# A fused encoder layer on one core: another order in the front, and more places for gate weights, projection weights and tanh tiles

## The chip, the cores and the metric

The kernel runs on one core of a Trainium2 chip. The metric is the device time of one execution in microseconds; times given are medians of several executions. A core has TensorE (PE in the profile), VectorE (DVE), ScalarE (ACT), GpSimd (POOL) and SyncE (SP). Each takes its own instructions in the order in which they were written for it; they wait for each other by semaphores. SP and ACT also issue the transfers (DMA): an issue is an instruction in that engine's order, and what stands behind it waits until the issue may go out.

## What is computed

One layer of a streaming encoder in fp32, for 1024 prompt rows and 8 x 16 sampled rows together (1152 rows of 1024):

```python
z = rmsnorm(x) @ w_in                       # q,k,v of branches a and b, q of m, forget gate, 3 x 1024 gates
a: band attention, 8 heads x 64, bias by distance
b: forgetting attention, 8 heads x 64, logit[t, s] += sum of log sigmoid(forget gate)
m: cross attention to 256 memory tokens, 4 heads x 128
x += (sum over branches of sigmoid(gate) * (branch @ w_p)) @ w_o
x += relu(rmsnorm(x) @ w_up) ** 2 @ w_down
```

It returns the layer's output, the normed keys, the values and the log forget gates.

## The kernel before

Each fp32 operand of a matmul is split in a hi part (rounded to fp32r, mostly by ScalarE) and a lo part (the difference, mostly by VectorE), and each product is three matmuls: hi by hi, hi by lo, lo by hi. Before a product can start on TensorE, its weight or left side must be loaded raw, copied to hi, and subtracted to lo.

The stages in order of time:

- **Front (0 to 75 us).** x is loaded transposed in five tiles of 256 rows (the fifth, tile 4, of 128; its output tile is number 8, `TT - 1`) into an arena FE (`x_place`, `x_load`, L375 to L381), split (`x_split`, L383), and multiplied with the weights of branch a's values and of the forget gate (loop at L750). `x_place` has two places of 2048 columns that take turns, and one of 1024 for tile 4. Beside it the rows of x are loaded once more, 512 KB at a time, into FE from column 4096, and squared and summed by ScalarE for the norm (`row_sums`, L393; `x_rows`, L399). After every second output tile, `sums` (L421) adds halves of x for the products that follow, and only then does the code load, split and row-sum the next tile.
- **Input projections (75 to 369 us).** q, k, v of a and b and q of m in products that share sums of operands (seven in place of eight). Raw weights go through a ring of slots in an arena RW; `kept` are four of them that are loaded in the front.
- **Memory keys and values (356 to 390 us).** `mem_products` (L823) with two output tiles; `flush` runs what is due of delayed steps (`in_`, L558), and `odd_x` (L801) prepares the right side for later. `norm` (L593) squares, sums and scales the keys, `to_T` transposes them on TensorE.
- **Attention (395 to 1090 us).** Written by a planner (class `Plan`, L50): a heap of steps with estimated due times and costs for each engine. The order of all engines from here is what this plan comes to, so an added buffer or another estimate moves everything behind it. Attention to the prompt and to the samples, aa, sa, ab, sb, am, sm, is done in turn. Where TensorE would wait, the plan puts in filler: first `gates` (L936), 24 products with weights in_w_g over three column tiles of 384, whose tanh goes to a table tg in DRAM; then `merge`.
- **Gates' weights.** `staged` (L924) loads a weight with a DMA that ACT issues into a raw tile `wst`, copies hi (`whi`) and subtracts lo (`wlo`). There is one raw tile for the gates. `get(f + 1)` is called at the gate's second column tile (L965).
- **Merge (957 to 1172 us).** For each branch (a, b, m), eight weights in_w_p and three column tiles, four slices each: products `z<-hi,whi` with the attention output (oTa, oTb, oTm, read back by SP and split in `load` and `part`, L995 to L1014), multiplied with the tanh tiles `th`, which SP reads back from tg through three places (`tanhs`, L985). The weights go through a ring "st" of three. The first two weights are asked for once gate 22 has begun its last column tile (`weights`, L1050).
- **Forget gates.** `forget_gates` (L849): log sigmoid in some 25 small VectorE steps, a transpose (tp<-lf), two running sums, both to DRAM; branch b reads them from 650 us on.
- Then the output projection (1172 to 1280), and the MLP (up to 1650, down to 2009 us).

The wait of the merge's first weights and the one raw tile for the gates, as written:

```python
yield from plan.until(lambda: ("x", 22, 2) in late and "mf" in late)     # merge, weights()
def staged(pool, src, tiles, at, key, shape=(P, 512), ring=("wst", 1)):
wq = fil.enter_context(weights(1, 4, "wq", "right"))                     # one raw tile, four split ones
```

## Time and profile before

| | us |
|---|---|
| median of 3 runs | 2014.13 |
| lowest and highest | 2010.42, 2015.04 |
| profiled execution, its own time | 2010.68 |
| span of that execution in the trace | 2008.9 |
| mean granted clock of TensorE | 0.989 of full speed |

In the rows below, a row of a timeline is one instruction or several alike (x4): its start and duration in us, engine, line, operation, output and inputs by the program's names, and in brackets how long its engine was idle before it and whom it waited for. Most instructions carry the line of a helper (L203, L215, L222), so they are told by the names of the tiles. A row of DMA on a queue (SPq, ACTq) is the issue; when the data has landed is seen from the instruction that reads it. A window's row gives length, busy time of PE, PEld (weight loads), DVE, ACT and POOL, then the granted TensorE clock, the busy share of the DMA engines and what they moved.

### The profile page before, as it was taken

What the parts mean: (1) busy time and instruction counts of PE and PEld (TensorE: products, weight loads), DVE (VectorE), ACT (ScalarE), POOL (GpSimd) and SP (SyncE); (2) the same over time, 40 slices, a digit from 0 to 9 for tenths busy, and PEclk for the clock granted to TensorE, in tenths of its full rate; (3) what the DMA queues carried; (4) which work ended last, traced back from release to release, by engine and by line L of the source; (5) the groups of instructions that cost most, each with busy time, mean ns of one, the idle gap of its engine ahead of it and who ended that gap; (6) DMA issues with size and microseconds to landing.
All of it is one profiled execution on the core that took longest, in us unless ns stands there. A gap on an engine that the chain in (4) does not pass through costs nothing.

```text
span 2008.9 us, 33955 instructions
## 1 busy us (share of the span) xinstructions
PE 1954.7 (97%) x12338; PEld 1712.1 (85%) x12338; DVE 1221.4 (61%) x2313; ACT 946.0 (47%) x1831; POOL 521.1 (26%) x590
## 2 busy tenths in 40 slices
PE   8999999899999999998899999999999999999999
PEld 8887888788887988887898987889999998888887
DVE  7766657665632555522575843876666665785775
ACT  6645556455643556533452313644444454453332
POOL 3343433332311244311122200244443431000000
PEclk9999999999999999999898999999999999999999
DMA  8555455643259433278658453144343459563463
GB/s 264 162 156 180 117 168 150 203 152 102 80 164 316 154 104 98 68 245 278 196 179 282 153 162 113 46 157 157 127 141 129 143 169 330 183 197 106 128 197 126
DMA packets 223909, 330.54 MB, mean 165 GB/s; under 512 B 32357, under 2 KB 109302, under 8 KB 223742
## 3 DMA queue, kind: packets, MB, share of 16 engines
q1 hardware_dynamic: 166600, 270.44, 42.3%
q10 hardware_dynamic: 57142, 57.93, 8.7%
q8 instruction: 97, 1.59, 0.3%
q14 instruction: 70, 0.57, 0.1%
HBM read 243.11 MB, written 85.18 MB: 163 GB/s over the span
## 4 chain that ended last, share of the span: by engine, by line
PE 77%; DMA 10%; DVE 6%; ACT 2%; issue 2%; POOL 2%; SPq 1%; ACTq 0%; POOLq 0%; DVEq 0%
PE b L1863 36%; PE z L215 28%; PE tp L222 5%; PE tp L215 4%; PE s L215 4%; DMA wst<-in_w_g 2%; DMA th<-tg 1%; POOL fa L203 1%; DVE r L203 1%; DVE fa L203 1%; DVE lo L203 1%; DMA kd<-in_cak 1%; DMA fa<-in_w_up 1%; SPq L203 1%; DMA tg<-tg 1%
## 5 line engine op out<-in xcount | busy, mean ns | idle before, releaser
L1863 PE MATMUL b<-r 128*128 128x512 f32 (+2 forms) x2200 | 457.6, 357 | 4.2 <-ACT r L203 2.1
L1863 PEld LDWEIGHTS b<-r 128*128 128x128 f32 x2200 | 379.6, 190 | 62.6 <-DVE r L203 3.6
L203 ACT ACTIVATE r<-fa 128x512 fp32r<-128x512 f32 (+4 forms) x264 | 212.8, 816 | 327.2 <-PE b L1863 280.9
L203 DVE TENSOR_TENSOR r<-fa,r 128x512 fp32r<-128x512 f32 (+4 forms) x264 | 273.5, 1047 | 136.1 <-ACT r L203 131.9
L215 PE MATMUL z<-hi,whi 128*128 128x384 f32 x960 | 320.2, 365 | 15.0 <-ACT hi L203 8.0
L1863 PE MATMUL b<-r,r 128*128 128x320 f32 (+1 forms) x1928 | 288.3, 299 | 5.8 <-DVE r L203 5.7
L1863 PEld LDWEIGHTS b<-r,r 128*128 128x128 f32 x1928 | 271.2, 190 | 7.7 <-DVE r L203 7.7
L215 PE MATMUL z<-hi,wlo 128*128 128x384 f32 x768 | 262.0, 341 | 0.2
L203 POOL TENSOR_TENSOR fa<-fa 128x512 f32<-128x512 f32 x114 | 165.2, 1455 | 238.4 <-ACT fa L203 125.5
L215 PEld LDWEIGHTS z<-hi,whi 128*128 128x128 f32 x960 | 180.5, 193 | 39.4 <-issue 15.1
L215 PE MATMUL z<-wa,hi 128*128 128x512 f32 (+1 forms) x732 | 203.5, 365 | 6.4 <-ACT hi L203 4.7
L215 PE MATMUL z<-lo,whi 128*128 128x384 f32 x576 | 195.1, 339 | 0.0
L215 PEld LDWEIGHTS z<-wa,hi 128*128 128x128 f32 x732 | 128.7, 192 | 27.2 <-ACT hi L203 5.1
L215 PEld LDWEIGHTS z<-hi,wlo 128*128 128x128 f32 x768 | 146.7, 191 | 1.3 <-DVE wlo L203 1.3
L203 ACT ACTIVATE s<-s,nm 128x256 f32<-128x256 f32 (+8 forms) x180 | 121.2, 679 | 39.1 <-DVE nm L203 38.9
L203 POOL TENSOR_SCALAR s<-s,ri 128x256 f32<-128x256 f32 (+8 forms) x108 | 76.0, 709 | 232.1 <-DVE ri L203 208.7
L215 PE MATMUL z<-wa,lo 128*128 128x512 f32 (+1 forms) x366 | 130.5, 359 | 0.0
L203 DVE CUSTOM_DVE_ANT_0 s<-s,bias 128x384 f32<-128x384 f32 (+4 forms) x144 | 70.4, 526 | 84.3 <-PE s L215 81.3
L215 PEld LDWEIGHTS z<-lo,whi 128*128 128x128 f32 x576 | 109.8, 191 | 0.0
L222 PE MATMUL tp<-ident,s 128*128 128x128 f32 (+1 forms) x680 | 107.3, 277 | 1.7 <-ACT pt L203 1.2
L203 ACT ACTIVATE pt<-tp 128x256 f32<-128x256 f32 (+3 forms) x153 | 66.4, 454 | 80.6 <-PE tp L222 76.8
L203 DVE TENSOR_TENSOR fa<-b,fa 128x256 f32<-128x256 f32 (+1 forms) x160 | 70.5, 448 | 54.0 <-PE b L1863 39.1
(223 smaller groups left out, 3136.4 us busy)
## 6 DMA issues: line engine op xcount, KB each, us to landing
td<-fa SPq DMA_DIRECT2D x112, 256.0 KB
rw<-in_w_in SPq DMA_DIRECT2D x104, 256.0 KB
fa<-td SPq DMA_DIRECT2D x80, 256.0 KB
fa<-in_w_down SPq DMA_DIRECT2D x76, 256.0 KB
fa<-in_w_up SPq DMA_DIRECT2D x32, 512.0 KB
tg<-tg ACTq DMA_DIRECT2D x72, 192.0 KB
th<-tg SPq DMA_DIRECT2D x72, 192.0 KB
wst<-in_w_g ACTq DMA_DIRECT2D x48, 256.0 KB
```

What stands on the lines that cost most here:

```text
L203: ins = f(*a, **k)
L215: ins = nc.tensor.matmul(out, lhsT, rhs, **k)
L222: ins = nc.tensor.transpose(*a)
L1863: pin(nc.tensor.matmul(ps, lh, rh, **k))
```

## The change

In the front: a third place for x tiles (`t % 3`); the rows of x go to the arena RW, whose slots are not used yet, and to FE only for the last ones; tile 4 is loaded and split ahead of the first row sums; tile 2 is loaded, row-summed and split after output tile 0; the kept weights, rows 4 and 5, tile 3 and the first raw weights come after output tile 1. At the memory: the square goes to another tile; delays of 3 instead of 2; `odd_x` makes its parts with scaled splits, four ScalarE and four VectorE steps per tile, in steps 2 to 5 instead of at every second one. The forget gates start 30 us later by the plan, their VectorE estimate is 6 us instead of 3, the running sums are done in place. The gates have two raw tiles, and each asks for the next at its first column tile. The merge's first two weights have tiles of their own, and are asked for as soon as the pool "mf" is there; the tanh tiles have six places. The attention's twelve minima are columns of one tile.

```diff
@@ -375,7 +375,7 @@
         return FE[:, 4096:5120].rearrange("p (k t) -> p k t", k=8) if t == 4 else \
-            FE[:, t % 2 * 2048:t % 2 * 2048 + 2048].rearrange("p (k t) -> p k t", k=8)
+            FE[:, t % 3 * 2048:t % 3 * 2048 + 2048].rearrange("p (k t) -> p k t", k=8)
     def x_load(t, ks=slice(0, 8)):
@@ -391,7 +391,7 @@
     def row_sums(src, s, r, e):
-        xt = FE[:, 4096 + e * D:4096 + e * D + D]
+        xt = row[1][:, e * D:e * D + D]
         sp.dma_start(xt, src)
@@ -401,7 +401,7 @@
             row[0] = 1 - row[0]
-    row = [1]
+    row = [1, RW]
@@ -590,11 +590,11 @@
                 flush()
-    def norm(z, sc, dh, then, gain=None, fresh=False):
+    def norm(z, sc, dh, then, gain=None, fresh=False, lag=2):
         nh = HB // dh
         v3 = lambda t: t.rearrange("p (h d) -> p h d", h=nh)
-        sq = tl(pj, (P, HB), tag="sq", bufs=1)
+        sq = tl(pj, (P, 4, P), tag="zt").rearrange("p k t -> p (k t)") if fresh else tl(pj, (P, HB), tag="sq", bufs=1)
         act.activation(sq, z, AF.Square, scale=sc)
@@ -603,7 +603,7 @@
             gps.tensor_scalar(r[:, :nh], r[:, :nh], sc, 1.0, ALU.mult, ALU.mult)
-            in_(2, scale)
+            in_(lag, scale)
         def scale():
@@ -644,8 +644,8 @@
             sp.dma_start(o["mk"][t * P:(t + 1) * P, :], zn)
-            in_(2, lambda: to_T(zn, mkT, t))
-        norm(z, rm[:, t:t + 1], 128, then, g_of["km"], True)
+            in_(3, lambda: to_T(zn, mkT, t))
+        norm(z, rm[:, t:t + 1], 128, then, g_of["km"], True, 3)
     mem_v = v_out(o["mv"], rm, True)
@@ -721,12 +721,12 @@
         x_split(0, (k,))
-    x_rows(0)
-    sp.dma_start(bf, i["b_f"].to_broadcast((P, 8)))
     x_load(4)
     x_split(4)
+    x_rows(0)
     x_load(1, slice(0, 4))
     x_load(1, slice(4, 8))
+    sp.dma_start(bf, i["b_f"].to_broadcast((P, 8)))
     x_rows(1)
@@ -735,8 +735,6 @@
     makers.extend([take] * 16)
-    for k in range(4):
-        sp.dma_start(kept[k], rows_(Q_A)(k))
     sp.dma_start(ident, i["ident"])
@@ -762,21 +760,30 @@
         vec.scalar_tensor_tensor(lf[:, t, :], z[1][:, 252:260], rs[:, t:t + 1], bf, ALU.mult, ALU.add)
+        if t == 0:
+            x_load(2, slice(0, 4))
+            x_load(2, slice(4, 8))
+            x_rows(2, 3)
+            x_split(2)
         if t in (1, 3, 5):
...
                 step()
-            if t < 5:
-                x_load(t // 2 + 2, slice(0, 4))
-                x_load(t // 2 + 2, slice(4, 8))
-                x_split(t // 2 + 2)
-                x_rows(t + 1, t + 2)
             if t == 1:
+                for k in range(4):
+                    sp.dma_start(kept[k], rows_(Q_A)(k))
+                row[1] = RW[:, 6 * UW:]
+                x_rows(4, 5)
+                x_load(3, slice(0, 4))
+                x_load(3, slice(4, 8))
                 ask()
+                x_split(3)
             if t == 3:
+                row[1] = FE[:, 2048:4096]
                 x_rows(6, 7)
+    row[1] = FE[:, 4096:6144]
     for t in range(2):
         row_sums(i["mem"][t * P:(t + 1) * P, :], ss[:, TT + t:TT + t + 1], rm[:, t:t + 1], t)
-    T2, u2, u3 = ([FE[:, (4 * j + t) * HB:(4 * j + t + 1) * HB] for t in range(4)] for j in range(3))
+    u2, u3, T2 = ([FE[:, (4 * j + t) * HB:(4 * j + t + 1) * HB] for t in range(4)] for j in range(3))
     sp.dma_start(tri, i["tri"])
@@ -801,8 +808,9 @@
         x = kept[t].rearrange("p (k t) -> p k t", k=4)
-        vec.tensor_tensor(x, x, gcol[:, 0, 0:4, None].to_broadcast((P, 4, P)), ALU.mult)
-        into_odd(t, x)
+        h, l = odd(t)
+        for k in range(4):
+            hilo_scaled(x[:, k, :], h[:, k, :], l[k], gcol[:, 0, k:k + 1])
     def at_last(t):
@@ -831,10 +839,12 @@
             release(u0 + k)
-            if k % 2:
+            if u0 != 104:
                 flush()
-                if u0 == 104:
-                    odd_x(k // 2)
+            elif k % 2:
+                flush()
+            if u0 == 104 and 1 < k < 6:
+                odd_x(k - 2)
         for t in range(2):
@@ -848,6 +858,7 @@
     def forget_gates(pool):
+        yield plan.t + 30.0
         z = lf.rearrange("p t h -> p (t h)")
@@ -874,7 +885,7 @@
         vec.tensor_tensor(z, z, v, ALU.subtract)
-        yield plan.use("vec", 3.0)
+        yield plan.use("vec", 6.0)
         act.dma_start(o["lf"].rearrange("(t p) h -> p t h", p=P), lf)
@@ -893,16 +904,14 @@
         yield t_ + 1.0
-        cc = tl(pool, (8, NP), tag="cc")
-        vec.tensor_tensor_scan(cc, cp, cp, 0.0, ALU.add, ALU.bypass)
-        vec.tensor_scalar(cc, cc, -1.0, None, ALU.mult)
+        vec.tensor_tensor_scan(cp, cp, cp, 0.0, ALU.add, ALU.bypass)
+        vec.tensor_scalar(cp, cp, -1.0, None, ALU.mult)
         yield plan.use("vec", 3.0)
-        act.dma_start(ncp, cc)
-        cd = tl(pool, (DB * 8, NK), tag="cd")
-        vec.tensor_tensor_scan(cd, cs, cs, 0.0, ALU.add, ALU.bypass)
-        vec.tensor_scalar(cd, cd, -1.0, None, ALU.mult)
+        act.dma_start(ncp, cp)
+        vec.tensor_tensor_scan(cs, cs, cs, 0.0, ALU.add, ALU.bypass)
+        vec.tensor_scalar(cs, cs, -1.0, None, ALU.mult)
         yield plan.use("vec", 1.6)
-        act.dma_start(ncs, cd)
+        act.dma_start(ncs, cs)
     def halves(n):
@@ -921,7 +930,7 @@
         yield plan.op(k, n)
-    def staged(pool, src, tiles, at, key, shape=(P, 512), ring=("wst", 1)):
+    def staged(pool, src, tiles, at, key, shape=(P, 512), ring=("wst", 2)):
         w = yield from plan.ring(*ring)
@@ -962,7 +971,7 @@
                     ps = tl(psum["z"], (P, 512), tag="z")
-                    if (f, c) == (22, 0) or c == 1 and f < 22:
+                    if c == 0 and f < 23:
                         plan.spawn(get(f + 1), own=False)
@@ -980,14 +989,15 @@
             src = i["w_p" + order[x // 8]][x % 8].rearrange("p k f -> p (k f)")
-            yield from staged((wpool[0], late["mf"]), src, wt, at, ("w", x), ring=("st", 3))
+
+            yield from staged((late["mf"] if x < 2 else wpool[0], late["mf"]), src, wt, at, ("w", x), ring=("st", 3))
         def tanhs():
...
                 g0 = {"a": 0, "b": D, "m": 2 * D}[order[bi]] + f * P
-                w = yield from plan.ring("th", 3)
-                t = tl(late["mf"], (P, CH), tag="th", bufs=3)
+                w = yield from plan.ring("th", 6)
+                t = tl(late["mf"], (P, CH), tag="th", bufs=6)
                 sp.dma_start(t, tg[g0:g0 + P, c * CH:(c + 1) * CH])
@@ -1002,7 +1012,7 @@
                     w = yield from plan.ring(*ring)
-                    st = tl(pool, (P, 512), tag=tag, bufs=ring[1])[:, :CH]
+                    st = tl(pool, (P, 512 if pool is late["mf"] else CH), tag=tag, bufs=ring[1])[:, :CH]
                     sp.dma_start(st, src[:, k, :])
@@ -1049,7 +1059,7 @@
                 for x in range(2):
-                    yield from plan.until(lambda: ("x", 22, 2) in late and "mf" in late)
+                    yield from plan.until(lambda: "mf" in late)
                     plan.spawn(get(x), own=False)
@@ -1777,7 +1790,7 @@
     fil = ExitStack()
-    wq = fil.enter_context(weights(1, 4, "wq", "right"))
+    wq = fil.enter_context(weights(2, 4, "wq", "right"))
     late = {}
```

How the order moves, at three places.

**ScalarE, in the front, behind the last value weight.** hi_163 and hi_164 are the hi parts of x tile 4, the 128x1024 step is the Square of a row sum, zn the output of tile 0, sa sums of halves. Before:

```order
L203 ACTIVATE sb_264<-rw_252 128x520
L203 ACTIVATE fe_268,ss_243<-fe_268 128x1024
L203 ACTIVATE sa_260<-fe_268 128x512
L203 ACTIVATE zn_476<-z_426,rs_241 128x260
L203 ACTIVATE zn_476<-z_451,rs_241 128x252
L203 ACTIVATE hi_163_231<-fe_268,gcol_201 128x128 x4
L203 ACTIVATE hi_164_232<-fe_268,gcol_201 128x128 x4
L203 ACTIVATE hi_143_211<-fe_268,gcol_201 128x128 x4
```

Now:

```order
L203 ACTIVATE sb_264<-rw_252 128x520
L203 ACTIVATE hi_163_231<-fe_268,gcol_201 128x128 x4
L203 ACTIVATE hi_164_232<-fe_268,gcol_201 128x128 x4
L203 ACTIVATE rw_252,ss_243<-rw_252 128x1024
L203 ACTIVATE hi_143_211<-fe_268,gcol_201 128x128 x4
L203 ACTIVATE hi_153_221<-fe_268,gcol_201 128x128
L203 ACTIVATE hi_144_212<-fe_268,gcol_201 128x128 x4
L203 ACTIVATE hi_153_221<-fe_268,gcol_201 128x128 x3
```

The hi parts of tile 4 come first, then the Square; tile 1's parts (hi_143, hi_144, hi_153) follow, and the outputs zn come later.

**TensorE, end of the memory products.** z_3696 and z_3697 (now 3704, 3705) are the memory values, tp the transposes of the normed keys, z_3839 (3840) the first gate. Before:

```order
L215 MATMUL z_3696<-wa_256,sa_260 128x512 x3
L215 MATMUL z_3697<-wa_256,sa_260 128x512 x3
L215 MATMUL z_3696<-wa_256,sa_260 128x512 x3
L215 MATMUL z_3697<-wa_256,sa_260 128x512 x3
L222 MATMUL tp_3785<-ident_203,zn_3747 128x128 x4
L222 MATMUL tp_3793<-ident_203,zn_3751 128x128 x4
L215 MATMUL z_3839<-hi_143_211,whi_3775 128x384
```

Now:

```order
L215 MATMUL z_3704<-wa_256,sa_260 128x512 x3
L215 MATMUL z_3705<-wa_256,sa_260 128x512 x3
L222 MATMUL tp_3769<-ident_203,zn_3743 128x128 x4
L222 MATMUL tp_3777<-ident_203,zn_3747 128x128 x4
L215 MATMUL z_3704<-wa_256,sa_260 128x512 x3
L215 MATMUL z_3705<-wa_256,sa_260 128x512 x3
L215 MATMUL z_3840<-hi_143_211,whi_3799 128x384
```

The transposes stand ahead of the last pair of products instead of behind it.

**ScalarE and SP, towards the merge.** w_pa are the merge's weights, w_g the last gate's; wst<-oTa slices of attention output, th<-tg tanh tiles. ScalarE, before (from its row 1046) and now (from its row 1020):

```order
L203 ACTIVATE spt_11023<-tp_11024 128x512
L203 DMA wst_11044<-in_w_pa 128x512
L203 DMA wst_11054<-in_w_pa 128x512
L203 ACTIVATE t_2114_10048<-tp_11048 16x128
L203 ACTIVATE hi_2279_10941<-wst_11030 128x384
L203 ACTIVATE whi_11046<-wst_11044 128x512
L203 ACTIVATE of_11098<-tp_11070 128x128
L203 ACTIVATE whi_11056<-wst_11054 128x512
L203 ACTIVATE tg_11141<-tg_11141 128x384
```

```order
L203 ACTIVATE t_1925_9864<-tp_10433 16x128
L203 DMA wst_10441<-in_w_g 128x512
L203 DMA wst_10446<-in_w_pa 128x512
L203 DMA wst_10450<-in_w_pa 128x512
L203 ACTIVATE tg_10457<-tg_10457 128x384
L203 DMA tg_76<-tg_10457 128x384
L203 ACTIVATE of_10502<-tp_10463 128x128
L203 ACTIVATE whi_10443<-wst_10441 128x512
L203 ACTIVATE whi_10448<-wst_10446 128x512
L203 ACTIVATE whi_10452<-wst_10450 128x512
```

The first two weights go out right behind the last gate's and are split some 22 rows earlier. SP, before and now:

```order
L203 DMA wst_11092<-oTa_71 128x384
L203 DMA th_11131<-tg_76 128x384
L203 DMA wst_11133<-oTa_71 128x384
L203 DMA th_11137<-tg_76 128x384
L203 DMA th_11139<-tg_76 128x384
L203 DMA wst_11144<-oTa_71 128x384
L203 DMA ld_11166<-qTm_68 128x1024
L203 DMA wst_11195<-oTa_71 128x384
L203 DMA th_11200<-tg_76 128x384
L203 DMA wst_11210<-oTa_71 128x384
```

```order
L203 DMA wst_10902<-oTa_71 128x384
L203 DMA wst_10926<-oTa_71 128x384
L203 DMA th_10954<-tg_76 128x384
L203 DMA th_10964<-tg_76 128x384
L203 DMA th_10967<-tg_76 128x384
L203 DMA th_10974<-tg_76 128x384
L203 DMA th_10976<-tg_76 128x384
L203 DMA th_10981<-tg_76 128x384
L203 DMA wst_10998<-oTa_71 128x384
L203 DMA wst_11006<-oTa_71 128x384
```

Six tanh tiles stand together ahead of the last two slices of oTa, where three and two stood among the slices.

## Rows read from the trace of the kernel before

**Rows 1.** The page, parts 1 and 6: busy time of the engines; a kind of load.

```profile
PE 1954.7 (97%) x12338; PEld 1712.1 (85%) x12338; DVE 1221.4 (61%) x2313; ACT 946.0 (47%) x1831; POOL 521.1 (26%) x590
...
th<-tg SPq DMA_DIRECT2D x72, 192.0 KB
```

**Rows 2.** The waits of TensorE: for what, us in total, times, longest.

```profile
PE z L215 <- ACT hi L203: 12.7, 5, 3.6
...
PE z L215 <- ACT whi L203: 4.5, 3, 3.0
...
PE z L215 <- DVE th L203: 3.4, 4, 1.0
...
PE tp L222 <- DVE zn L203: 2.8, 2, 1.7
...
PE tp L222 <- DVE lf L203: 1.8, 1, 1.8
...
PE tp L222 <- ACT pt L203: 1.2, 1, 1.2
```

**Rows 3.** Windows: length, busy time of each engine (count), clock, DMA share, GB/s.

```profile
19.00:29.00 10.00, 7.45 (x48) 7.08 (x47) 9.90 (x29) 8.65 (x27) 1.55 (x2) 0.83 0.79 261
41.00:48.00 7.00, 4.87 (x28) 4.67 (x27) 5.04 (x11) 6.67 (x16) 0.96 (x3) 0.76 1.06 395
375.00:400.00 25.00, 18.59 (x81) 15.38 (x80) 16.42 (x45) 6.34 (x11) 4.81 (x11) 0.86 0.50 170
400.00:900.00 500.00, 493.95 (x3854) 420.17 (x3853) 244.42 (x799) 258.91 (x622) 142.87 (x224) 1.00 0.46 146
900.00:930.00 30.00, 24.73 (x226) 19.15 (x226) 8.00 (x27) 8.07 (x19) 4.56 (x10) 0.94 0.93 310
962.00:977.00 15.00, 8.93 (x29) 7.14 (x29) 4.64 (x9) 5.43 (x10) 1.31 (x1) 0.66 0.65 218
1052.00:1066.00 14.00, 10.59 (x66) 6.82 (x68) 5.16 (x10) 3.54 (x9) 0.48 (x1) 0.63 1.03 400
1100.00:1175.00 75.00, 70.92 (x396) 68.17 (x396) 60.52 (x101) 24.84 (x46) 19.49 (x15) 1.00 0.53 163
```

**Rows 4.** Timeline of ScalarE, 18 to 28: start us, duration us, instruction [idle before].

```profile
18.24 1.06 ACT L203 ACTIVATE fe<-fe 128x1024 f32<-128x1024 f32 x1 [1.43 <-DMA fe<-in_x]
...
21.98 6.24 ACT L203 ACTIVATE hi<-fe,gcol 128x128 fp32r<-128x128 f32 x21
```

**Rows 5.** Timeline of VectorE, front: the row sums ahead of the small tile.

```profile
20.01 1.42 DVE L203 TENSOR_TENSOR fe<-fe 128x512 f32<-128x512 f32 x2
```

**Rows 6.** Timeline of SP, front: the issue of the third x tile.

```profile
36.14 1.29 SPq L203 DMA_DIRECT2D fe<-in_xT  x2
```

**Rows 7.** Timeline of ScalarE at the memory products.

```profile
372.43 0.38 ACTq L203 DMA_DIRECT2D wst<-in_w_g  x1
...
377.37 0.63 ACT L203 ACTIVATE whi<-wst 128x512 fp32r<-128x512 f32 x1 [2.56 <-DMA wst<-in_w_g]
```

**Rows 8.** Timeline of ScalarE in the sampled rows of branch b.

```profile
918.17 0.36 ACTq L203 DMA_DIRECT2D wst<-in_w_g  x1
...
924.33 0.63 ACT L203 ACTIVATE whi<-wst 128x512 fp32r<-128x512 f32 x1 [4.68 <-DMA tg<-tg]
```

**Rows 9.** Timeline of ScalarE at the start of the merge.

```profile
960.30 0.34 ACTq L203 DMA_DIRECT2D wst<-in_w_pa  x1
...
963.94 0.52 ACT L203 ACTIVATE hi<-wst 128x384 fp32r<-128x384 f32 x1 [2.73 <-DMA wst<-oTa]
...
967.67 0.63 ACT L203 ACTIVATE whi<-wst 128x512 fp32r<-128x512 f32 x1 [3.21 <-DMA wst<-in_w_pa]
...
968.73 0.51 ACT L203 ACTIVATE hi<-wst 128x384 fp32r<-128x384 f32 x1
```

**Rows 10.** Timeline of ScalarE where the merge turns to branch b.

```profile
1047.28 0.39 ACTq L203 DMA_DIRECT2D wst<-in_w_pb  x1
...
1053.14 0.63 ACT L203 ACTIVATE whi<-wst 128x512 fp32r<-128x512 f32 x1 [4.84 <-DMA wst<-in_w_pb]
```

More of the change, by code (lines that the diff above doesn't have):

```diff
@@ L1100, in prompt_ab @@
         turned, summed = defaultdict(int), defaultdict(dict)
-        live, softs = [0], [0]
-        pvs = set()
+        live, softs, count = [0], [0], [0]
+        least = tl(pool, (P, 12), tag="nm", bufs=1)
         def prepare(p):
@@ L1177, in soften @@
                 off = BAND - nkey if b == "a" else 0
-                nm, was = tl(pool, (P, 1), tag="nm", bufs=12), nms.get(e)
+                j = count[0] % 12
+                count[0] += 1
+                nm, was = least[:, j:j + 1], nms.get(e)
                 vec.tensor_tensor_reduce(s[:, x:x + m], ps[:, :m], bias[:, off + x:off + x + m], -1.0,
```

## The prediction

> **What bounds the kernel now.** I read the page's first part: TensorE is busy for 1954.7 us of a span of 2008.9 us, VectorE for 61% and ScalarE for 47% [rows 1]. Nothing in the change takes a matmul away, so what can be won is the 54.2 us in which TensorE is idle, and the time in which it runs at half clock. The waits of TensorE come next: what it waits for most is a hi part that ScalarE has to make (12.7 us in only 5 waits), then the hi part of a weight (4.5 us in 3), the tanh tiles read back (3.4 us in 4), the normed memory keys (2.8 us) and the forget gates (1.8 us) [rows 2]. Few and long waits are edges between stages, so windows around the edges say what each costs: its length less TensorE's busy time is idle, and one less the granted clock, times the length, is what the half level (1.2 of 2.4 GHz) took beside it. The reader is to see that the clock is below 1 just at these edges, and 1.00 in the 500 us of attention between them [rows 3].
>
> From rows 3, idle + clock:
> - front, first place (19 to 29): 2.55 + 1.70 = 4.25 us
> - front, second place (41 to 48): 2.13 + 1.68 = 3.81
> - memory products and first gates (375 to 400): 6.41 + 3.50 = 9.91
> - attention (400 to 900): 6.05 + 0
> - sampled rows of b (900 to 930): 5.27 + 1.80 = 7.07
> - start of the merge (962 to 977): 6.07 + 5.10 = 11.17
> - its turn to branch b (1052 to 1066): 3.41 + 5.18 = 8.59
> - rest of the merge (1100 to 1175): 4.08 + 0
>
> Together 54.9 us. What lies behind 1175 is not touched.
>
> **The change part by part.**
>
> *Front.* At 18.24 ScalarE begins a Square of 1.06 us that had waited for a row load, and the hi parts of the small tile, for which TensorE stands still, follow at 21.98 [rows 4]. Now these hi parts and their load come first. They can't help before the lo parts are there: VectorE keeps the row sums ahead of them, which end at 21.43 [rows 5], so of the wait, which ends at 22.43, about 1.0 us goes and 1.5 stays. With the shorter wait I count half of the clock's 1.7. The second wait is for x tile 2, issued only at 36.14 [rows 6], because its place was free only after the sums of tile 0. With three places it is issued right behind the first output tile: all 3.8 us go. Against this, the output of tile 0 now stands behind two Squares of the row sums (2 x 1.06 us); two banks lie between it and TensorE, so I charge 0.6, with bounds of 0 and 2.1. The kept weights and the first raw weights are issued later, but are needed only at 75 us, so they cost nothing; were they late by as much as x tile 2, it would be its 3.8. Front: -1.9 - 3.8 + 0.6 = **-5** (-8 to -2).
>
> *Memory products.* Here ScalarE issues a gate weight at 372.43 and reads it at 377.37, 4.94 us later, with the hi part of the last memory weights behind it [rows 7]. Both gate weights are now issued together behind the last of these, the two transposes of the normed keys stand ahead of the last pair of products, so that 1.4 us of matmul cover a wait of 1.7, and the forget gates' chain (TensorE waited 1.8 us for it [rows 2]) starts 30 us later among gates that cover it. The extra ScalarE work (16 small hi parts instead of 4 large ones) is paid for by VectorE's saved multiplications. I leave 1 us: **-9** (-10 to -5).
>
> *Attention.* Two raw gate weights let the next one be fetched while this one is split. The 6.05 us are a dozen waits of at most 1.2 us, few of them for weights: **-1.5** (-3 to 0). The twelve minima in one tile change no work.
>
> *Sampled rows of b.* A gate weight issued at 918.17 reaches its split at 924.33 [rows 8], and TensorE waits 3.0 us [rows 2] and loses clock. With a second raw tile it is issued a gate step earlier, which is more than the 6.2 us of the flight. The loads run at 310 GB/s there [rows 3], and may land later: **-5** (-7 to 0).
>
> *Start of the merge.* A projection weight issued at 960.30 is split at 967.67, and the hi part of the attention output that TensorE needs stands behind it on ScalarE at 968.73 [rows 9]. The slice before it was late by itself: ScalarE sat idle 2.73 us for it until 963.94. The first two weights are now asked for some 35 ScalarE rows earlier, in places of their own; this cures the late slice, since it lets the loads spread. But the third weight is still issued at the merge's start, and its split still stands ahead of the last slices, which on SP are now behind six tanh tiles. One of these is 192 KB [rows 1], 0.90 us at 218 GB/s [rows 3], so six are 5.4 us. I leave 2.5 us of wait and 2.2 of clock: 11.2 - 4.7 = **-6.5** (-11 to 0).
>
> *Turn to b.* The same pattern: a weight issued at 1047.28 is split at 1053.14, with a hi part behind it [rows 10]. Slices and weight now stand ahead of the memory keys and values on SP: 8.6 less 2.6 that I leave: **-6** (-8.6 to 0).
>
> *Tanh tiles.* Six places instead of three let them be read ahead; 3.4 of 4.1 us are waits for them [rows 2, 3]: **-3** (-4 to -1).
>
> *What the new order costs.* All of the plan behind 390 us comes out in another order, so other small waits will appear. The nearest row is one wait for a transposed probability tile of 1.2 us [rows 2]; I take four: **+5** (0 to +12).
>
> Sum: -5 - 9 - 1.5 - 5 - 6.5 - 6 - 3 + 5 = **-31 us**. On the profiled execution's 2010.68 this is 1979.7. The median shown is 2014.13, 3.4 above that execution, so I forecast **1983 us**. All terms at their best give -51.6 and 1962.5; all at their worst +4 and 2018.
>
> **A rule weighed.** At the turn to b the DMA engines are busy for 1.03 of the window at 400 GB/s, at the sampled rows 0.93 at 310 [rows 3]: there the loads fill the engines. The Trainium skill, "DMA: Bandwidth & Descriptors", section "Issuing engines are not separate DMA queues", says that transfers started from different engines run on the same 16 DMA engines and interleave, and that starting them side by side saves only the sequencer's issue time. By that rule an earlier issue in these two stretches would win little more than nothing, and the sum would be that of the first rival; the trace agrees as to the turn to b, while at the start of the merge a share of 0.65 leaves room.
>
> **The rivals.**
> 1. *The loads fill the engines.* What is issued earlier makes others late, and waits with their clock stay at the sampled rows and at the turn to b, and half of them at the merge's start: 5 + 6 + 3.2 = 14 us less. -17 us, **1997 us**. For it the two shares above; against it that the stretches are short and 400 to 900 has a share of only 0.46 [rows 3], into which the earlier issues reach.
> 2. *The merge's edges don't change.* The split of the third weight still stands ahead of the last slices, six tanh tiles too, and the order hides nothing else: the terms of the merge (6.5 + 6 + 3) are gone. -15.5 us, **1998.5 us**. For it the order of ScalarE and SP; against it that the first slices and weights are there earlier.
> 3. *Slower: the tanh tiles run ahead of the weights.* Three more of them in flight put 3 x 0.90 = 2.7 us ahead of each of the 24 projection weights; if none of it were covered, it would be 65 us, if two thirds of it were not, 43: **2026 us**. It decides where a weight has less lead than its flight of 7.4 us [rows 9] and this 2.7. The merge takes some 215 us for 24 weights (960 to 1175), 9 us each, and asks two ahead: a lead of 18. So it can bite at the edges, hardly between them.
> 4. *No change:* the new order's waits eat the gains, some 26 more waits of 1.2 us [rows 2]: 2014 us. Against it, all of 400 to 900 has only 6.05 us idle now, in the same planner's hands.
>
> **How the numbers follow.** The forecast has 0.64, rival 1 has 0.15, rival 2 has 0.09, rival 3 has 0.07, rival 4 has 0.05. About 0.2% (4 us) is what a measurement of this kernel can tell from no change. Faster by more is forecast and rivals 1 and 2: 0.88; within it rival 4: 0.05; slower 0.07. The range reaches from near the best sum to rivals 1 and 2 with the upper bound of the new waits: **1964 to 2005 us**.
>
> **What would show it.** Right: in windows around 44 and 385 us the clock at 1.00 and idle under 1 and 2 us; no wait over 1 us for a hi part of a gate or projection weight between 900 and 1070, but one of 2 to 3 us at the merge's third slice; waits for tanh tiles under 1 us in all. Busy time of TensorE some 13 us lower, the share of the clock in the terms, since a matmul at half clock is busy for longer. The forecast is wrong if the clock still falls at three of the edges, if the DMA share at 900 to 930 and at the turn to b is again near 1 with waits for weights, or if 400 to 900 shows far more than 6 us of idle.

## The result, and the profile after

The changed kernel takes **1986.7 us** (median of 4 runs, 1983.51 to 1989.88), beside 2012.67 us of the kernel before on the same chip: a ratio of 0.9871 with a 95% interval of 0.9848 to 0.9893, so 22 to 31 us faster. The forecast was 1983 us, the range 1964 to 2005. The profiled execution took 1988.38 us, its span is 1986.6 us.

The page's busy time, which answers to [rows 1]:

```profile
PE 1947.7 (98%) x12338; PEld 1709.6 (86%) x12338; DVE 1226.1 (62%) x2305; ACT 949.1 (48%) x1844; POOL 535.1 (27%) x593
```

The span is 22.3 us shorter, TensorE's busy time 7.0 us less, at a mean granted clock of 0.994 for 0.989. The waits of TensorE, which answer to [rows 2]:

```profile
PE s L215 <- DMA kd<-in_cak: 3.5, 3, 1.9
...
PE z L215 <- ACT hi L203: 2.4, 2, 1.7
...
PE z L215 <- ACT whi L203: 1.3, 1, 1.3
...
PE tp L222 <- DVE lf L203: 1.1, 1, 1.1
...
PE z L215 <- DVE th L203: 1.0, 1, 1.0
```

The reader is to see that 12.7 us of waits for a hi part have become 2.4, the weights' 4.5 have become 1.3 and the tanh tiles' 3.4 have become 1.0, and that ahead of the output projection something else now leads: cached keys of branch a, whose loads land late. (Over the whole span the longest entry is one that the prediction left out, DVE's r in the MLP: 7.7 us before, 7.4 now.)

To see where the time went, the two traces are cut at the same events of the program: the first product of the input projections (at 68.3 us before, not the 75 of the list of stages), the 24th pair of gate products, the sampled rows of b, the first merge product, and so on. The columns are those of [rows 3]. Before:

```profile
0.00:68.30 68.30, 62.02 (x460) 61.01 (x461) 49.16 (x102) 47.34 (x107) 19.47 (x28) 0.95 0.81 258
68.30:423.70 355.40, 346.32 (x1627) 282.43 (x1626) 241.91 (x429) 186.97 (x331) 136.00 (x161) 0.99 0.53 159
423.70:863.00 439.30, 435.52 (x3425) 369.18 (x3423) 220.85 (x735) 235.66 (x566) 130.73 (x206) 1.00 0.42 135
863.00:957.60 94.60, 88.25 (x828) 73.86 (x824) 26.50 (x79) 31.44 (x73) 13.47 (x28) 0.98 0.87 276
957.60:987.60 30.00, 23.93 (x122) 22.09 (x121) 14.80 (x29) 10.38 (x26) 2.37 (x2) 0.83 0.58 185
1032.00:1085.40 53.40, 49.99 (x384) 42.68 (x383) 26.94 (x59) 16.70 (x40) 6.24 (x8) 0.90 0.80 284
1085.40:1172.40 87.00, 82.92 (x496) 79.96 (x494) 67.91 (x111) 28.67 (x54) 25.31 (x20) 1.00 0.55 171
1172.40:2004.90 832.50, 821.24 (x4728) 738.09 (x4728) 538.65 (x708) 360.25 (x556) 177.40 (x132) 1.00 0.47 153
```

After:

```profile
0.00:61.60 61.60, 57.99 (x460) 57.26 (x461) 49.40 (x103) 47.83 (x108) 24.05 (x28) 1.00 0.87 276
61.60:409.20 347.60, 344.43 (x1655) 282.90 (x1654) 232.95 (x410) 191.78 (x348) 138.46 (x163) 1.00 0.55 165
409.20:849.10 439.90, 433.73 (x3391) 366.14 (x3390) 230.49 (x749) 233.24 (x563) 130.91 (x204) 1.00 0.42 135
849.10:942.10 93.00, 89.13 (x828) 75.91 (x827) 27.43 (x80) 31.17 (x72) 14.22 (x27) 0.98 0.88 281
942.10:972.10 30.00, 27.02 (x142) 25.48 (x139) 13.33 (x25) 8.53 (x21) 3.27 (x3) 0.89 0.69 215
1018.10:1073.70 55.60, 53.30 (x426) 47.74 (x425) 33.04 (x65) 18.10 (x44) 10.11 (x12) 1.00 0.84 290
1073.70:1145.50 71.80, 70.79 (x426) 69.24 (x425) 60.74 (x99) 26.12 (x50) 21.26 (x16) 1.00 0.55 166
1145.50:1982.60 837.10, 825.19 (x4729) 740.58 (x4728) 538.76 (x710) 362.04 (x558) 179.53 (x132) 0.99 0.47 153
```

Worked out as in the prediction, idle (length less TensorE's busy time) and clock (one less the granted clock, times the length; from the unrounded clock):

| stretch | before | after | change | forecast |
|---|---|---|---|---|
| front, up to the first projection | 9.7 | 3.6 | -6.1 | -5 |
| memory products and first gates | 12.5 | 3.2 | -9.3 | -9 |
| attention up to the samples of b | 3.8 | 6.2 | +2.4 | -1.5, and most of +5 |
| samples of b, up to the merge | 8.1 | 5.6 | -2.5 | -5 |
| first 30 us of the merge | 11.2 | 6.4 | -4.8 | -6.5 |
| its turn to b | 8.5 | 2.3 | -6.2 | -6 |
| rest of the merge | 4.1 | 1.0 | -3.1 | -3 |
| output projection and MLP | 14.7 | 18.7 | +4.0 | 0 |
| sum | 72.5 | 47.0 | -25.5 | -31 |

The output projection starts 26.9 us earlier (1145.5 for 1172.4). The last row of the table is code that the change doesn't touch. It varied between executions of all kernels from 11 to 19 us, mostly by how often the clock fell between short waits there, so 4 us of the difference between forecast and profile are put down to the execution.

The losses fell by 25.5 us and the span of the same two executions by 22.3: the other 3.2 us are busy time at full clock, 1939.6 us for 1936.4, which the table leaves out. What took them is open.

Each column is one execution. The changed kernel was profiled a second time (an experiment below). Three of its stretches, the front, attention and the samples of b:

```profile
0.00:67.40 67.40, 60.59 (x460) 59.01 (x460) 48.51 (x101) 46.39 (x106) 25.24 (x28) 0.97 0.78 251
...
416.50:859.10 442.60, 434.50 (x3391) 366.57 (x3390) 229.45 (x749) 233.51 (x563) 131.28 (x204) 1.00 0.41 134
859.10:950.00 90.90, 87.24 (x828) 74.29 (x828) 28.61 (x81) 31.90 (x73) 13.95 (x27) 1.00 0.89 291
```

Down the table, that profile holds 8.5, 4.2, 9.8, 3.7, 3.8, 2.2, 1.0 and 15.4 us, in sum 48.6. So the sum is much the same, while an entry can differ by 2 to 5 us between two executions of one program. Entries of a single profile are to be read with that in mind, here and in the experiments.

### The profile page after: what moved, and what is told of

Same layout as the page of the kernel before. It is cut to its first block, busy times and chain, and to the rows that moved or that the text cites. A ratio compares the mean times of both kernels' runs of the same rounds, so it can differ in the third digit from the quotient of the medians.

```text
span 1986.6 us, 33937 instructions
## 1 busy us (share of the span) xinstructions
PE 1947.7 (98%) x12338; PEld 1709.6 (86%) x12338; DVE 1226.1 (62%) x2305; ACT 949.1 (48%) x1844; POOL 535.1 (27%) x593
## 5 line engine op out<-in xcount | busy, mean ns | idle before, releaser
L215 PE MATMUL z<-hi,whi 128*128 128x384 f32 x960 | 315.4, 361 | 5.2 <-ACT hi L203 2.4
L203 POOL TENSOR_SCALAR s<-s,ri 128x256 f32<-128x256 f32 (+8 forms) x103 | 69.6, 680 | 244.8 <-DVE ri L203 204.0
```

What stands on the lines that cost most here:

```text
L203: ins = f(*a, **k)
L215: ins = nc.tensor.matmul(out, lhsT, rhs, **k)
```

## The experiments

All undo parts of the change, or add to it (the diffs are against the changed kernel), and were timed beside the kernel before. Its median was 2010.44 us on the chip of the first four, 2007.15 for the next four, 2008.78 for the last four, so ratios are compared. A ratio's interval is some 0.2% to either side, and that of a difference of two ratios some 0.3%, or 6 us: time alone tells no part of 2 to 5 us from nothing, and what the single runs decide they decide by the edges of one profile each.

**The front as before.**

```diff
-            FE[:, t % 3 * 2048:t % 3 * 2048 + 2048].rearrange("p (k t) -> p k t", k=8)
+            FE[:, t % 2 * 2048:t % 2 * 2048 + 2048].rearrange("p (k t) -> p k t", k=8)
...
+    x_rows(0)
     x_load(4)
     x_split(4)
-    x_rows(0)
...
-        if t == 0:
-            x_load(2, slice(0, 4))
```

> The front as it was before, all else as changed. Theory (each edge stands for itself): both waits and both stretches of half clock in the first 50 us come back, the products start some 6.7 us later (68.3 instead of 61.6), all behind keeps its order and distance, and the time is about 7 us above the changed kernel's 1986.7. Rival (what the front saves is given back later, since something behind it waits for a fixed time, such as a load): the products start 6.7 us later, but the output projection starts less than 3 us later.

1993.27 us, ratio 0.9908 (0.9881 to 0.9935). Both waits are back, as the timeline of TensorE shows:

```profile
22.62 0.75 PE L215 MATMUL z<-wa,hi 128*128 128x260 f32 x4 [2.57 <-ACT hi L203]
...
44.09 0.89 PE L215 MATMUL z<-wa,hi 128*128 128x260 f32 x5 [2.27 <-ACT hi L203]
```

The projections start at 69.5 us, the output projection at 1154.0 for 1145.5: 8.5 us later. Beside the changed kernel's second profile (67.5 and 1150.2) it is 2.0 and 3.8 us. By the ratios the time is 7.4 us longer, with 7 to either side. In neither comparison is what the front saves given back, so the rival falls; the theory's 7 us fit, but are not known better than that.

**The memory products as before.**

```diff
-            in_(lag, scale)
+            in_(2, scale)
...
-            if u0 == 104 and 1 < k < 6:
-                odd_x(k - 2)
+                if u0 == 104:
+                    odd_x(k // 2)
```

> The memory products as before (shorter delays, sums of the odd half by one multiplication each, all queued steps flushed at every second product), the rest as changed. Theory: waits for the normed keys and the half clock near 375 us come back, 5 to 8 us between the start of the products and the first gates; time +5 to +8. Rival (the delayed forget gates alone cured this edge, because VectorE and ScalarE were full of their steps): under 2 us.

1986.66 us, ratio 0.9886 (0.9864 to 0.9907). The edge (memory products and first gates) went from 3.2 to 7.8 us, within the expected; but the first 30 us of the merge had 2.0 instead of 6.4, and the output projection started 1.2 us earlier than in the changed kernel. The edge is as expected. The time is 3 us above the changed kernel's by the ratios, with 6 to either side, so neither the theory's 5 nor the rival is decided by it; that the plan, written anew, gave back elsewhere what the edge lost is how this one profile reads, and is not shown.

**One raw tile for the gates.**

```diff
-    wq = fil.enter_context(weights(2, 4, "wq", "right"))
+    wq = fil.enter_context(weights(1, 4, "wq", "right"))
...
-                    if c == 0 and f < 23:
+                    if (f, c) == (22, 0) or c == 1 and f < 22:
```

> One raw tile for the gates' weights, asked for at the second column tile as before; the rest as changed. Theory (the second raw tile hides the flight of a weight): waits for whi come back in the two stages of sampled rows (600 and 900 us), and one of 3 us with half clock near 915; time +4 to +8. Rival (there the loads fill the engines, so issuing earlier gains nothing): within 2 us of the changed kernel.

1988.66 us, ratio 0.9896 (0.9873 to 0.9918): 5 us above by the ratios with 6 to either side, so told apart neither from the changed kernel nor from the theory's +4 to +8. The edge at the first gates is 9.5 us (1.7 of them a clock drop at 65.4 us that belongs to the front), with a wait for a gate weight:

```profile
398.17 0.44 PE L215 MATMUL z<-hi,whi 128*128 128x384 f32 x1 [3.35 <-ACT whi L203]
```

but the samples of b have 5.7 us, as with two raw tiles (5.6, and 3.7 in the second profile). So the second tile pays at the first gates, and at the samples of b, where I had put its 5 us, no gain from it is seen. The changed kernel's own timeline of ScalarE says why:

```profile
899.53 0.64 ACT L203 ACTIVATE whi<-wst 128x512 fp32r<-128x512 f32 x1 [2.40 <-DMA wst<-in_w_g]
...
901.17 0.37 ACTq L203 DMA_DIRECT2D wst<-in_w_g  x1
...
901.94 1.50 ACTq L203 DMA_DIRECT2D wst<-in_w_pa  x2
...
907.11 0.63 ACT L203 ACTIVATE whi<-wst 128x512 fp32r<-128x512 f32 x1 [1.51 <-DMA wst<-in_w_g]
```

Each gate's weight comes in two halves, and by the code (`get` in `gates`) the second half is asked for only when the first is split, with one raw tile or with two. The weight in question is the second half of the last gate's. It goes out 1.64 us behind the split of the first half (899.53). In the kernel before it was 1.38 us, from this row to the 918.17 of [rows 8]:

```profile
916.79 0.63 ACT L203 ACTIVATE whi<-wst 128x512 fp32r<-128x512 f32 x1 [3.48 <-DMA wst<-in_w_g]
```

From split to split it is 7.58 us now and was 7.54. So the second raw tile could not bring this weight's issue forward. (And the last gate's weight was asked for at the first column tile before as well, by L965.) In the changed kernel it is also followed on the queue by the merge's two first weights, and is split 5.9 us after its issue.

**The merge's first weights as before.**

```diff
-            yield from staged((late["mf"] if x < 2 else wpool[0], late["mf"]), src, wt, at, ("w", x), ring=("st", 3))
+            yield from staged((wpool[0], late["mf"]), src, wt, at, ("w", x), ring=("st", 3))
...
-                    yield from plan.until(lambda: "mf" in late)
+                    yield from plan.until(lambda: ("x", 22, 2) in late and "mf" in late)
```

> The merge's first two weights without places of their own, asked for only once gate 22 is in its last column tile; the rest as changed. Theory of the prediction: the edge at the merge's start (6 us of wait and half clock now) grows again to some 9 to 11 us, time +3 to +5. Rival (at that edge TensorE waits for the last slices of attention output, not for weights): waits there are the same within 1 us, and the time within 2 us, or even less since two loads fewer compete with the last gate's weight.

1987.32 us, ratio 0.9882 (0.986 to 0.9905), not told apart. In the profile the edge grew to 11.3 us (before: 11.2), as the theory had it, and the output projection starts 5.6 us later. The waits of TensorE at the merge's start:

```profile
950.14 0.45 PE L215 MATMUL z<-hi,whi 128*128 128x384 f32 x1 [3.70 <-ACT hi L203]
...
954.64 0.69 PE L215 MATMUL z<-hi,whi 128*128 128x384 f32 x1 [1.40 <-ACT hi L203]
```

and the last slices of attention output on SP, by its timeline:

```profile
945.41 0.32 SPq L203 DMA_DIRECT2D wst<-oTa  x1
...
951.19 0.32 SPq L203 DMA_DIRECT2D wst<-oTa  x1
```

The merge began at 939.7, so these slices went out 5.7 and 11.5 us behind its first product. TensorE waits for slices, as the rival said, but their lateness follows the weights': by the code a weight on its way holds one of three raw places that weights and slices share, and the kernel with a later third weight, below, bears that out for one of two slices.

The last gate's weight, without the merge's first weights behind it, is split 3.9 us after its issue here:

```profile
901.11 0.37 ACTq L203 DMA_DIRECT2D wst<-in_w_g  x1
...
905.02 0.63 ACT L203 ACTIVATE whi<-wst 128x512 fp32r<-128x512 f32 x1 [1.03 <-DMA wst<-in_w_g]
```

With them behind it, it took 5.9 and 5.7 us in the changed kernel's two profiles. The samples of b lose 2.7 us here, for 5.6 and 3.7: in these profiles asking early for the merge's weights has a price there.

**Three places for tanh tiles.**

```diff
-                w = yield from plan.ring("th", 6)
-                t = tl(late["mf"], (P, CH), tag="th", bufs=6)
+                w = yield from plan.ring("th", 3)
+                t = tl(late["mf"], (P, CH), tag="th", bufs=3)
```

> Three places for tanh tiles as before, the rest as changed. Theory: the waits for tanh tiles in the last 75 us of the merge come back (3 us), while at the merge's start only three tiles instead of six stand ahead of the last slices, so that edge shrinks from 6.4 us to about 4; in sum within 2 us of the changed kernel. Rival of the prediction (more tanh tiles in flight make weights late): the middle of the merge gets better by more than 2 us, and the time is 3 us or more below the changed kernel.

1982.61 us, ratio 0.9875 (0.9855 to 0.9895). The merge's last stretch has 3.5 us instead of 1.0 and its turn to b 4.3 instead of 2.3, while its first 30 us have 1.1 instead of 6.4. In sum the same time, as expected: in these profiles six tanh tiles give 4.5 us late in the merge and take 5.3 at its start (2.7 beside the second profile's 3.8). The rival, tanh tiles ahead of weights in the middle of the merge, falls: the waits for them only come back.

**The forget gates without the delay.**

```diff
-        yield plan.t + 30.0
...
-        yield plan.use("vec", 6.0)
+        yield plan.use("vec", 3.0)
```

> The forget gates start at once and with the old estimate of 3 us, the rest as changed. Theory (the delay, beside the second raw tile and the memory part, cures the edge of the first gates): idle and half clock in the first 35 us of the gates go from 0.6 to 3 or 4 us, with a wait of 1 to 2 us for the forget gates' transpose; time +2 to +4. Rival (the other two parts suffice): under 1 us there.

1980.61 us, ratio 0.9860 (0.9834 to 0.9886). The wait is there again:

```profile
389.20 0.30 PE L222 MATMUL tp<-ident,lf 128*72 128x128 f32 x1 [1.56 <-DVE lf L203]
```

and the first 35 us of the gates lose 1.9 us for 0.6, between the theory's 3 to 4 and the rival's 1. But the whole edge is 4.0 us, 0.8 above the changed kernel's first profile and no more than its second (4.2), and the time is not above it. With the other two parts in place, no gain from the delay is seen.

**Tanh tiles held back; and the third weight later.** Two kernels, the second with both edits:

```diff
-                yield from plan.until(lambda: bi < len(order))
+                yield from plan.until(lambda: bi < len(order) and (bi or len(th) < 2 or "sliced" in late))
...
+                    if (b, c, k) == ("a", NC - 1, 3):
+                        late["sliced"] = 0
...
-                    for y in {(4, 0): (2, 3), (5, 0): (3,), (6, 0): (), (7, 0): (), (7, 2): (2,)}.get((f, c), (2,) if c == 0 else ()):
+                    for y in {(0, 0): (), (0, 2): (2,), (4, 0): (2, 3), (5, 0): (3,), (6, 0): (), (7, 0): (), (7, 2): (2,)}.get((f, c), (2,) if c == 0 else ()):
```

> As changed, but only two tanh tiles are read until the last slice of branch a's attention output has been issued. Theory A (at the merge's start the six tanh tiles delay the last two slices on SP): the slices land some 3 us earlier, idle and half clock in the merge's first 30 us fall from 6.4 to under 3, time -3 to -4. Theory B (the slices wait for a free raw place, which the third weight holds): the edge stays at 5 to 7 us.

> As the kernel with held tanh tiles, and the merge's third weight is asked for two column tiles later, so that a raw place is free for the last slices. Theory A: no better than the kernel with held tiles alone, or worse by up to 2 us if the third weight is then late. Theory B: the edge falls under 3 us only here, time -3 to -4 against the changed kernel.

In the changed kernel the merge begins at 942.1. Its timeline of ScalarE, where TensorE's waits of 1.75 and 0.66 us end:

```profile
942.74 0.37 ACTq L203 DMA_DIRECT2D wst<-in_w_pa  x1
...
948.34 0.63 ACT L203 ACTIVATE whi<-wst 128x512 fp32r<-128x512 f32 x1 [3.55 <-DMA wst<-in_w_pa]
...
949.16 0.52 ACT L203 ACTIVATE hi<-wst 128x384 fp32r<-128x384 f32 x1 [0.19 <-DMA wst<-oTa]
...
951.40 0.52 ACT L203 ACTIVATE hi<-wst 128x384 fp32r<-128x384 f32 x1 [1.72 <-DMA wst<-oTa]
```

and of SP:

```profile
940.38 2.80 SPq L203 DMA_DIRECT2D th<-tg  x6
945.49 1.29 SPq L203 DMA_DIRECT2D wst<-oTa  x2
```

The third weight's split (948.34) is in front of a slice, as I had forecast, but the slices themselves have only just landed (949.16), or not yet (951.40, 1.72 us idle for the load): they were issued 3.4 us behind the merge's first product, behind six tanh tiles. With these held, on SP:

```profile
951.43 0.90 SPq L203 DMA_DIRECT2D th<-tg  x2
956.45 1.29 SPq L203 DMA_DIRECT2D wst<-oTa  x2
```

The merge begins at 953.1 there: the slices go out 3.4 us behind it, as late as ever, but land faster, and the edge is 2.1 us. (The samples of b lose 10.8 us in this profile, with nothing changed there.) With the third weight later as well:

```profile
934.52 0.91 SPq L203 DMA_DIRECT2D th<-tg  x2
936.72 3.14 SPq L203 DMA_DIRECT2D wst<-oTa  x2
```

The merge begins at 936.3, the first of the slices goes out 0.4 us later, the second 3.2 (4.4 in the changed kernel), and the edge is 2.0 us. So both theories have a part in these profiles: the issue is late for want of a raw place (B, seen in the issue of the first slice), the landing is late behind the tanh tiles' traffic (A), and with the landing cured the edge is small. That either edit did it is not shown: with the memory part undone or with one raw tile the edge is 2.0 and 1.6 us without them. In time, the first gives 1977.22 us, ratio 0.9862 (0.9824 to 0.9900), the second 1981.53, 0.9864 (0.9838 to 0.9889), both below the changed kernel's 0.9871, but within its interval. So the second was run again, beside the changed kernel itself:

> The changed kernel itself, so that it stands on the same chip as the next one. Every theory: 0.987 of the kernel before, and in the profile the same order of instructions; stretches up to 1145 us that differ between executions are put down to transfers.

> The kernel with held tanh tiles and the later third weight, timed beside the changed kernel. Theory (the slices of branch a were late for want of a raw place and behind tanh tiles): 3 to 6 us below the changed kernel in the median. Rival (what its profile showed was one good execution): within 2 us.

The changed kernel: 1983.72 us, ratio 0.9871 (0.9850 to 0.9892), the same as the first time. With both edits: 1984.95 us, 0.9889 (0.9867 to 0.9911). Its edge is cured in this profile too (2.5 us), but the changed kernel's was 3.8 this time instead of 6.4, with the slices issued 2.0 and 2.9 us behind the merge's first product instead of 3.4 and 4.4, and no gain in time is shown. No version was found that beats the change.

The changed kernel's second profile shows something else. In the front ScalarE stood still:

```profile
52.01 0.84 ACT L203 ACTIVATE zn<-z,rs 128x260 f32<-128x260 f32 x2 [5.73 <-DMA out_va<-zn]
```

In its first profile the same step (the output of a value tile, into a place from which an earlier one is being written out) waited for other things:

```profile
44.93 0.84 ACT L203 ACTIVATE zn<-z,rs 128x260 f32<-128x260 f32 x2 [1.97 <-POOL rs L203]
```

The wait of 5.73 us is for the landing of a store. Behind it stands the split of x tile 3, TensorE waits 2.34 us and loses clock, and the projections start at 67.5 us instead of 61.6. The transfers in that stretch of the second profile, as windows:

```profile
34.00:42.00 8.00, 8.00 (x70) 8.00 (x69) 8.00 (x19) 7.21 (x16) 4.70 (x1) 1.00 1.01 368
42.00:52.00 10.00, 8.96 (x76) 8.75 (x74) 3.70 (x8) 2.52 (x6) 3.95 (x8) 1.00 0.92 308
```

Of the twelve profiles of kernels with the new front (the changed kernel's two, and ten others), seven start the projections between 61.3 and 62.3 us, and five between 63.9 and 67.5. That same step waits for the store in eleven of the twelve: 2.90 to 5.73 us in the five late ones, 1.27 to 3.64 in six of the others. Two of these, with 3.08 and 3.64 us, start their projections before 62 us all the same, so a wait of some 3 us is mostly covered.

**Memory products and forget gates as before; and one raw tile as well.** The edits of the single kernels together; the last two lines are in the second kernel alone.

```diff
-            in_(lag, scale)
+            in_(2, scale)
...
-        yield plan.t + 30.0
...
-    wq = fil.enter_context(weights(2, 4, "wq", "right"))
+    wq = fil.enter_context(weights(1, 4, "wq", "right"))
```

> Memory products and forget gates as before (no delay, the old estimate), two raw tiles and all else as changed. Theory (each part bears on the edge at the first gates, and they add): idle and half clock from the start of the products to the 24th pair of gate products, 3.2 us in the changed kernel, 7.7 with the memory part alone undone, go to 9 or more; time +5 or more. Rival (the planner's new order behind the edge gives or takes as much as the edge itself): the edge is 8 or more, but the time stays within 2 us.

> As the kernel with memory and forget gates as before, and also one raw tile for the gates: only the front, the merge's first weights and the tanh tiles are left of the change. Theory: the edge at the first gates is back at the 12.5 us of before, the sampled rows of b at 8 us, and the start of the merge, its turn to b and the tanh waits stay cured; time +10 to +13 against the changed kernel. Rival (the middle parts give nothing in sum): within 3 us.

The first: 1988.12 us, ratio 0.9893 (0.9873 to 0.9914); its edge is 11.1 us (1.7 of them again a clock drop of the front, at 66.9 us), but attention has 3.8 instead of 6.2 and the merge's start 4.6 instead of 6.4. The edge is there. The time is 4.4 us above the changed kernel's on the same chip, with 6 to either side: the theory's 5 and the rival's 2 are not told apart. The second: **2004.87 us, ratio 0.9976 (0.9961 to 0.9990)**, 1.05% or 21 us above the changed kernel, more than the 10 to 13 expected, and 16.8 us above the first, from which it differs by the raw tile alone. Its windows for four stretches (first gates, samples of b, merge's first 30 us, turn to b):

```profile
61.70:414.10 352.40, 345.63 (x1626) 283.43 (x1624) 241.20 (x428) 186.62 (x330) 138.62 (x161) 0.99 0.53 162
...
853.90:949.40 95.50, 89.22 (x829) 75.22 (x826) 28.26 (x81) 32.04 (x74) 13.23 (x27) 0.96 0.87 280
...
949.40:979.40 30.00, 25.28 (x140) 23.76 (x140) 16.04 (x31) 11.43 (x28) 3.75 (x4) 0.89 0.60 193
...
1021.10:1074.10 53.00, 48.74 (x383) 42.49 (x382) 25.77 (x56) 16.93 (x42) 7.03 (x8) 0.94 0.83 293
```

They hold 10.2, 9.7, 8.1 and 7.7 us of idle and clock. The first two were expected; that the merge's edges come back too, with their own parts of the change still there, was not. This profile is of the fastest of ten executions (1994.35 us), while the two of the changed kernel are of its longer ones (1988.38 and 1989.72), so its losses, 56.5 us for 47.0 and 48.6, are no measure of the 21 us: of these, 8 to 10 us at most are seen in a profile. The eight executions above 2000 us have granted clocks of 0.990 to 0.994, on average 0.992 for the profiled one's 0.993, so only some 2 of their 10 us more are half clock. What the rest is was not seen.

## Why the prediction was right

**The bound.** TensorE's idle time and half clock at a few edges were what could be won, and there it was won: of 72.5 us 25.5 went. That the median fell by 26.0 agrees so closely by luck: the span of the two profiled executions fell by 22.3.

**Front (-5).** -6.1 in the profile, 6.7 us by the start of the projections, 7 us (0.4 to 14) by the ratios of the run that undoes it; but -1.2 in the second profile. The first wait kept 1.38 us, for lo parts, as worked out; its clock didn't fall at all, where I had counted half. The charge of 0.6 us for the output of tile 0 wasn't seen, but in five of twelve profiles the projections start 2 to 6 us later, with a wait for a store's landing ahead of x tile 3, a step that I hadn't priced.

**Memory products and first gates (-9).** -9.3, and -8.3 in the second profile. Right as a sum over three parts. By the single runs, and without the clock drops that belong to the front, the parts are worth 4.6 (memory), 4.6 (raw tile) and 0.8 us (forget gates) at this edge, 6.2 for memory and forget gates together, and 7.0 for all three: the raw tile gives 4.6 us alone and 0.8 on top of the others. Parts that cure the same wait stand in for each other.

**Samples of b (-5).** The term that was most mis-sized in the first profile: -2.5 (-4.4 in the second). The step that failed is "With a second raw tile it is issued a gate step earlier": the weight that TensorE waited for is a gate's second half, which is asked for behind the split of the first half whatever the raw tiles, and it went out 1.64 us behind that for 1.38. With one raw tile the stretch was no worse (5.7 us). Which part of the new order gave the 2.5 us is open. Against them, the merge's first weights, asked for earlier by another part of the same change, now share that weight's flight (5.9 and 5.7 us with them, 3.9 without). The window from 849 to 942 us is at 281 GB/s with a DMA share of 0.88. The Trainium skill, "DMA: Bandwidth & Descriptors", section "Issuing engines are not separate DMA queues", has the transfers of all issuing engines run on the same 16 DMA engines and interleave. That an earlier issue therefore wins little was the prediction's conclusion; no run here tests it at the samples of b, where the issue didn't move, and the turn to b, where the prediction had the trace agree, goes against it with -6.2.

**Start of the merge (-6.5).** -4.8, and -7.4 in the second profile. What I had left for it, 2.5 us of wait and 2.2 of clock, came out at 3.0 and 3.4. Of the two causes that I gave for it, the slices behind six tanh tiles are the nearer one: the third weight's split does stand ahead of a slice, but that slice landed only 0.19 us after the split was done.

**Turn to b (-6), tanh tiles (-3).** -6.2 and -3.1, and the same in the second profile. No run undoes the turn to b alone: it holds 4.3 us with three tanh tiles, 5.6 without the early first weights and 7.7 with three other parts undone, so which part cures it is not shown.

**New order (+5).** Attention rose by 2.4 us to 6.2 (9.8 in the second profile), of which 3.5 are waits for cached keys, where I had counted a gain of 1.5 and new waits of 5: +3.5, between the two. The sign of what a new order does in one place is not to be foretold from here: the merge's first 30 us lost 1.6 us with one raw tile and 8.1 with three parts undone, none of them at that place.

**The rivals.** The loads' limit (1997 us): not at the turn to b, and at the samples of b the waits that stay have another reason beside it, the issue. Unchanged edges of the merge: no, -4.8 and -6.2. Tanh tiles ahead of the weights: seen only at the start and only ahead of slices, at 5 us in one comparison and 3 in the other. No change: no.

**The signs.** The clock stayed up in the front and at the memory products, and fell at two edges, not three. But busy time fell by 7.0 us, not 13 (10.2 us of half clock went, and 3.2 us of busy time at full clock came); a wait of 1.28 us for a gate weight's hi part stayed at 908 us; the wait at the merge's third slice was 1.75 us, not 2 to 3; and the tanh tiles' waits were 1.0 us, at the bound.

What stays open: why the merge's edges come back when memory part, delay and raw tile are undone together, and where the slower executions of that kernel lose 10 us more. So of the 26 us, the edges in the profiles are shown, and in time the three middle parts together and, just, the front; the merge's two parts moved no time when undone singly. And whether a third place for the value outputs would end the scatter of the front was not tried.

## What to carry to other kernels

Where one engine is busy 97% of the time, add up its idle time and its half clock over stretches between the same events of the program, not over the same times: the sum bounds what any reordering can give, and after it shows which edge paid. Take it from more than one profile: here single stretches differed by up to 5 us between two executions of the same program. Parts that cure the same edge don't add, so undo them together before saying what one is worth. Before pricing an earlier issue, look in the code at what the issue waits for: a second place for a weight is no help where the weight's second half is asked for behind the split of its first. Where weights and operands share a ring of raw places, look at when the operand's load is issued, not only at what stands ahead of its split.

## What was not expected of the hardware

A store of 256 KB issued by ScalarE landed so late, while loads moved 308 to 368 GB/s, that ScalarE idled 5.73 us for the place it held; in the other profiled execution of the same program the same step didn't wait for it at all. Executions of the changed kernel on one chip spread from 1973.67 to 1989.72 us, 0.8%, those of the kernel before from 2005.23 to 2014.98, 0.5%.
